# Weight sums of a Strassen-form MLP: one step per head behind a norm's power, in place of a fixed grid, and two sets moved from the recurrence to the first MLP

## The chip, the cores and the metric

The kernel runs on one core of a Trainium2 chip. The metric is the device time of one execution in microseconds (us), here the median of several runs. The names of the engines in profile rows: PE is TensorE (matmuls), PEld its weight loads, DVE is VectorE, ACT is ScalarE, POOL is GpSimd, SP is SyncE. DMAs are issued here by SP (queue q1 in the DMA view) and by POOL (queue q0); only POOL issues DMAs that add to what stands at their destination. A row like "L538" names line 538 of the kernel before; line 204 is a helper that issues every operation whose cost the kernel's planner counts, so L204 rows are told apart by their tiles.

## What is computed

One sequence of 1024 tokens, width 1024, runs through two layers: a gated linear recurrence with eight heads, an MLP of width 4096 with a squared ReLU, a causal convolution module, and a second such MLP, each followed by a layer norm of the weighted residual sum. All of it is float32.

```python
for i in range(DEPTH):                       # DEPTH = 2
    if i == 0: mix = hgrn2_mixer(x, ...)     # recurrence, 8 heads of 128
    else:      mix = conformer_conv_mixer(x, ...)
    x = layer_norm(ALPHA * x + mix, ...)
    ff = square(relu(x @ ffn_w1[i])) @ ffn_w2[i]
    x = layer_norm(ALPHA * x + ff, ...)
```

Within the recurrence each head's output is normed before it is gated: `o * rsqrt(mean(o*o) + RMS_EPS)`, per token and head.

## The kernel before

Matmuls are made of float32 operands cut into a high and a low part, three matmuls for each pair. The large products also use a Strassen form: a product of 2 x 2 blocks is made from seven products (`ORDER` lists them) of sums of blocks instead of eight. This takes sums of the weights' blocks. For the second matrix of each MLP (`ffn_w2`, cut into eight chunks per layer, each of four blocks of 128 x 1024) the sums are made in DRAM, by DMAs, long before the chunk is used. One **set** is the sums of one chunk, four tiles of 0.5 MB named sum_w. It takes two copies of 1 MB (`v[:, 0:2]` and `v[:, 2:4]`), one add of 1 MB onto the first two tiles, and two chained adds of 0.5 MB, each of which adds the tile before it to the next, so that each of the three adds can start only when an earlier DMA has landed. 4 MB are moved in a set. The list `to_sum` holds the sixteen sets, the eight of layer 0 first; layer 0's down product reads its sums from about 860 us on (dr<-sum_w), layer 1's at the end of the kernel.

The recurrence is written as one hand-made order for all engines. An outer loop goes over twelve pairs of projection blocks (`PAIRS`), seven products (`ORDER`) each, twelve matmuls a product; after each three matmuls `slot()` moves a counter of ticks on. Work is put off with `later(n, job)`: the job is recorded n ticks on, on whatever engines it uses. Between the products a generator per head, `recurrence(h)`, is stepped, so that a head's small matmuls stand between the large ones. Each head ends thus: `settle(0)` and `settle(1)`, one for each half of the tokens, take squares and their sums on ACT (L755), a scale and the power -1/2 on POOL (L756, then L538 in `power_m_half`), and, four ticks later, the scaling on ACT (L761), whose result PE transposes. Each engine works its instructions off in the order in which they are recorded. A DMA that POOL issues waits there until what it reads has landed, and all that is recorded behind it on POOL waits too.

In this kernel sets are given out by position: at every sixth product (`(7 * p + ORDER.index(i)) % 6 == 1`, L1042) while more than four sets are left, `block_sums` records the first copy, the second copy six ticks later, and the add and the two chained adds 12, 24 and 36 ticks later (`gap=12`). That gives twelve sets to the recurrence. Their lines are L419 and L420 (copies), L421 (add) and L423 (chained adds). Two more sets are made in the first MLP, after chunks 0 and 2, in seven pieces, one behind each form's product (`sum_pieces`): there the four tiles are copied one at a time by SP (L435), each behind a DMA of one element that holds it until the form is cut (L434), and the three adds are POOL's (L440). The last two are made in the second MLP (L413, L415).

The last head (7) has no tiles of its own for its values: it loads them into the halves of the finished tile F, named f, in the middle of its recurrence (`load_values(2 * h, F...)`, issued by SP at L652), while the earlier heads load theirs two heads ahead (tile v). The matmuls `ps<-f,kt` and `ps<-f,at` take f. Around this `seam()` loads the first matrix of the output projection (w_out, SP, L960, tile raw, cast at L952) and the stored heads (back<-zd, u<-od).

After the recurrence the order is no longer made by hand (`order.close()`): a scheduler that models the engines sets it. In the first MLP, `Forms.ahead(3)` keeps three cut forms of the weights (tile fw) ahead of PE; ACT casts the high part (L72), VectorE makes the low one. Beside this `spare` prepares later weights: POOL's one-element copies L1464 and L1472 gate the use of a tile that ACT casts (L1465, spare<-next), and SP stores the result (ready<-spare).

Of the kernel before, what the change touches and what calls it, by code (L numbers as in the profile page):

```python
# [8 lines left out]
F32 = mybir.dt.float32  # L9
# [3 lines left out]
ALU = mybir.AluOpType  # L13
PSUM = bass.MemoryType.PSUM

P = 128
# [3 lines left out]
H = 8  # L20
# [24 lines left out]
ORDER = (1, 2, 6, 5, 7, 3, 4)  # L45
# [223 lines left out]
def body(ctx, tc, d, out):  # L269
    nc = tc.nc  # L270
    cst = ctx.enter_context(tc.tile_pool(name="cst", bufs=1))
    stat = ctx.enter_context(tc.tile_pool(name="stat", bufs=4))
    dram = ctx.enter_context(tc.tile_pool(name="dram", bufs=1, space=bass.MemoryType.DRAM))
# [110 lines left out]
    def later(n, job):  # L384
        if n:
            waiting.append((ticks[0] + n, job))
        else:
            job()

    def tick(n=1):  # L390
        for _ in range(n):
            ticks[0] += 1
            for at, job in [w for w in waiting if w[0] <= ticks[0]]:
                waiting.remove((at, job))
                job()

    sums = {}

    def block_sums(name, layer, c, after=None, gap=0, adds=None):

        t = sums[name, layer, c] = dram.tile([4, P, 1024], F32, name=f"sum_{name}{layer}{c}")
        v, w = t.rearrange("a p n -> p a n"), d[name][layer, c].rearrange("a p n -> p a n")
        queue = nc.sync if after is not None else nc.gpsimd
        if adds is not None:

            def copies(rows, after):
                nc.sync.dma_start(out=t[0:4:2, rows.start, 0:1], in_=after)
                queue.dma_start(out=v[rows, 0:2], in_=w[rows, 0:4:2])
                queue.dma_start(out=v[rows, 2:4], in_=w[rows, 0:2])

            copies(slice(16, P), after)
            adds.append(lambda after: copies(slice(0, 16), after))
            adds.append(lambda after: nc.gpsimd.dma_start(out=v[:, 0:2], in_=w[:, 2:4], accum_op=ALU.add))  # L413
            for i in (2, 3):
                adds.append(lambda after, i=i: nc.gpsimd.dma_start(out=v[:, i], in_=v[:, i - 1], accum_op=ALU.add, max_dma_last_dim=4096))  # L415
            return
        if after is not None:
            nc.sync.dma_start(out=t[0:4:2, 0, 0:1], in_=after)
        queue.dma_start(out=v[:, 0:2], in_=w[:, 0:4:2])  # L419
        later(gap // 2, lambda: queue.dma_start(out=v[:, 2:4], in_=w[:, 0:2]))  # L420
        parts = [lambda: nc.gpsimd.dma_start(out=v[:, 0:2], in_=w[:, 2:4], accum_op=ALU.add)]  # L421
        for i in (2, 3):
            parts.append(lambda i=i: nc.gpsimd.dma_start(out=v[:, i], in_=v[:, i - 1], accum_op=ALU.add, max_dma_last_dim=4096))  # L423
        for i, part in enumerate(parts):
            later((i + 1) * gap, part)

    def sum_pieces(name, layer, c):

        t = sums[name, layer, c] = dram.tile([4, P, 1024], F32, name=f"sum_{name}{layer}{c}")
        v, w = t.rearrange("a p n -> p a n"), d[name][layer, c].rearrange("a p n -> p a n")  # L430

        def copy(i, q):
            def go(after):
                nc.sync.dma_start(out=t[i : i + 1, 0, 0:1], in_=after)  # L434
                nc.sync.dma_start(out=v[:, i], in_=w[:, q])  # L435

            return go

        def add(out, x, **kw):
            return lambda after: nc.gpsimd.dma_start(out=out, in_=x, accum_op=ALU.add, **kw)  # L440

        def chained(i):
            return add(v[:, i], v[:, i - 1], max_dma_last_dim=4096)

        return [copy(0, 0), copy(1, 2), add(v[:, 0:2], w[:, 2:4]), copy(2, 0), chained(2), copy(3, 1), chained(3)]

    to_sum = [(*of, c) for of in (("w2", 0), ("w2", 1)) for c in range(NFC)]
# [73 lines left out]
    for k in range(4):  # L521
        c = slice((k % 2) * HT, (k % 2 + 1) * HT)
# [14 lines left out]
    def power_m_half(dst, src, n):  # L537
        nc.gpsimd.tensor_tensor(out=dst, in0=src, in1=nhalf[:, :n], op=ALU.pow)  # L538
# [115 lines left out]
    def recurrence(h):  # L654
# [71 lines left out]
        for n in (32, 64):  # L726
            for s in range(0, n2, 2 * n):
                c, r = divmod(s, P)
# [22 lines left out]
        def settle(half):  # L751
            ss = stat.tile([P, 2, 4], F32, tag="ss", name="ss")
            cs = range(half * NTB, half * NTB + NTB)
            for c in cs:
                nc.scalar.activation(o[:, c], out_ps[:, c, :], AF.Square, scale=1.0 / QSCALE, accum_out=ss[:, 0, c % NTB : c % NTB + 1])  # L755
            nc.gpsimd.tensor_scalar(out=ss[:, 1], in0=ss[:, 0], scalar1=1.0 / P, scalar2=RMS_EPS, op0=ALU.mult, op1=ALU.add)  # L756
            power_m_half(ss[:, 0], ss[:, 1], 4)

            def rest():
                for c in cs:  # L760
                    nc.scalar.activation(o[:, c], out_ps[:, c, :], AF.Copy, scale=ss[:, 0, c % NTB : c % NTB + 1])  # L761
                later(1, lambda: ready.add(half))

            later(4, rest)
# [38 lines left out]
        def attend(cs):  # L803
            for c in cs:
                tensor.matmul(out_ps[:, c, :], A[:, c, :], values(c), start=True, stop=c == 0)
                if c:
                    tensor.matmul(out_ps[:, c, :], Q[:, c * P : (c + 1) * P], states[c], start=False, stop=True)
# [6 lines left out]
        later(1, lambda: (chain(range(NTB, nk)), settle(0)))  # L814
        yield
        attend(range(NTB, 2 * NTB))
        later(1, lambda: settle(1))
        if h < H - 2:
            for half in range(2):
                load_values(2 * h + 2 + half)  # L820
# [168 lines left out]
    def seam():  # L989
        plan = [  # L990
            (5, lambda: fetch(0, 0)), (15, lambda: split_w(0, 0, 136)), (17, lambda: split_w(0, 1, 144)), (19, lambda: split_w(0, 3, 120)),
            (21, lambda: split_w(0, 2, 152)), (13, lambda: heads_in(0, 0, 4, 32)), (19, lambda: heads_in(0, 4, 6, 32)),
            (24, lambda: split_heads(0, 0)), (26, lambda: split_heads(0, 2)), (29, lambda: split_heads(0, 4)),
            (16, lambda: bring(0)), (17, lambda: bring(1)), (27, lambda: last_in(H - 2, 0, sixth[0])), (36, lambda: last_in(H - 1, 0, lastly[0])),
            (21, lambda: heads_in(1, 0, 6, 64)), (38, lambda: split_heads(1, 0)), (41, lambda: split_heads(1, 2)), (44, lambda: split_heads(1, 4)),
            (25, lambda: fetch(1, 80)), (39, lambda: split_w(1, 0, 112)), (42, lambda: split_w(1, 1, 128)),
            (45, lambda: split_w(1, 2, 96)), (47, lambda: split_w(1, 3, 104)),
            (43, lambda: last_in(H - 2, 1, sixth[1])), (46, lambda: last_in(H - 1, 1, lastly[1])),
        ]
        for n, job in plan:  # L1000
            later(n, job)
# [25 lines left out]
    for p, (kind, j) in enumerate(PAIRS):  # L1027
        st = {"banks": dict(turn_of)}
        turn_of = {"z": turn_of["a"], "a": turn_of["b"], "b": turn_of["z"]}
        pace[1] = 0.0 if p == 0 else 0.6 if p < 3 else 0.5  # L1030
        if kind == "g" and p < len(PAIRS) - 1:
            to_load += [(2 * j, 0), (2 * j + 1, 1), (2 * j, 1), (2 * j + 1, 0)]
        if p == len(PAIRS) - 1:
            seam()
        for i in ORDER:
            if kind == "q" and i == 2:
                while any(a[0] <= j - 3 for a in active) or recs and recs[0] <= j - 3:
                    tick()
                    step()
            pair_product(p, i, made.pop(0), st)  # L1040
            later(2, make_form)
            if (7 * p + ORDER.index(i)) % 6 == 1 and len(to_sum) > 4:  # L1042
                block_sums(*to_sum.pop(0), gap=12)
        if kind == "q":
            later(4, lambda j=j: recs.append(j))
    early_out = ((0, 0), (1, 0), (2, 0))
# [9 lines left out]
    tick(100)  # L1056
    assert not waiting and not loaded and not to_load and not gates, (waiting, gates)
    order.close()
    oT = [o[0] for o in oT]


# [186 lines left out]
    class Up:  # L1248
# [14 lines left out]
        def settle(self, c):  # L1263

            for q in range(2):
                self.first(self.of[c], q)
# [224 lines left out]
    for c in range(NFC):  # L1491
        for i in ORDER[2 if c < 2 else 0 :]:
            (f,) = fw.take(1)
            fw.ahead(3)
            if (c, i) == (0, 7):
                bg.done()
            up.form(c, i, f)
            if summing:
                summing.pop(0)(f[:1, 1, :1].bitcast(F32))
        if c in (0, 2):  # L1500
            summing += sum_pieces(*to_sum.pop(0))
        if c == 0:
            up.settle(1)
            hold += [view(208, (2, 1024), F32, "spare"), view(216, (1024,), F32, "next")]
# [478 lines left out]
```

## Time and profile before

| what | value |
|---|---|
| time before, median of 3 runs | 2057.65 us (2055.35 to 2061.02) |
| the profiled execution's own time | 2057.38 us |
| its span, first to last instruction | 2055.6 us |
| granted clock of TensorE, mean | 0.998 |
| busy: POOL | 394.7 us, 405 instructions |
| DMA of SP's queue (q1) | 456.93 MB, 61.7% of 16 engines' span |
| DMA of POOL's queue (q0) | 58.72 MB, 12.3% |
| copies and adds of POOL from the weights, 1 MB each | 40, 10.8 us from issue to landing (median) |
| chained adds of POOL, 0.5 MB each | 32, 8.3 us |

How to read it: the profile is one execution, so sums are made against its own 2057.38 us, and the median of the runs is 0.27 us above that. PE's busy time is modelled, and a matmul's duration overlaps the next one's; idle time of PE is what an edit can gain. A row of waits tells which engine and tile waited for what: us in total, how often, the longest. A timeline row has start, duration, engine, line, operation, tiles, and in brackets the idle time before it with what ended it.

### The profile page before, as it was taken

What the parts mean: (1) busy time and instruction counts of PE and PEld (TensorE: products, weight loads), DVE (VectorE), ACT (ScalarE), POOL (GpSimd) and SP (SyncE); (2) the same over time, 40 slices, a digit from 0 to 9 for tenths busy, and PEclk for the clock granted to TensorE, in tenths of its full rate; (3) what the DMA queues carried; (4) which work ended last, traced back from release to release, by engine and by line L of the source; (5) the groups of instructions that cost most, each with busy time, mean ns of one, the idle gap of its engine ahead of it and who ended that gap; (6) DMA issues with size and microseconds to landing.
All of it is one profiled execution on the core that took longest, in us unless ns stands there. A gap on an engine that the chain in (4) does not pass through costs nothing. (4 is left out here: it accounts for less than half of the span.)

```text
span 2055.6 us, 29682 instructions
## 1 busy us (share of the span) xinstructions
PE 2024.2 (98%) x11144; PEld 1669.3 (81%) x11144; DVE 1488.7 (72%) x1978; ACT 1092.3 (53%) x1725; POOL 394.7 (19%) x405
## 2 busy tenths in 40 slices
PE   8999999999999999999999999999999999999998
PEld 7888887888788888888888888888888888888886
DVE  8698887877866665666557898889589666754456
ACT  5456565631654655444443776488615555443343
POOL 0112232111000000000001799079210000100002
PEclk9999999999999999999999999999999999999999
DMA  4788999942399786999998755487659778995542
GB/s 187 216 206 229 263 244 250 268 185 89 125 324 298 275 302 215 374 341 325 336 339 294 303 185 187 191 329 268 255 210 344 247 236 299 392 293 195 194 154 103
DMA packets 183120, 517.55 MB, mean 252 GB/s; under 512 B 17984, under 2 KB 49856, under 8 KB 181824
## 3 DMA queue, kind: packets, MB, share of 16 engines
q1 hardware_dynamic: 167488, 456.93, 61.7%
q0 software_dynamic: 15488, 58.72, 12.3%
q8 instruction: 87, 1.43, 0.3%
q14 instruction: 57, 0.47, 0.1%
HBM read 380.85 MB, written 201.85 MB: 283 GB/s over the span
## 5 line engine op out<-in xcount | busy, mean ns | idle before, releaser
L204 PE MATMUL ps<-dw,dh 128*128 128x512 f32 x2688 | 611.6, 389 | 0.9 <-ACT dh L72 0.7
L204 PEld LDWEIGHTS ps<-dw,dh 128*128 128x128 f32 x2688 | 504.1, 188 | 106.3 <-ACT dh L72 1.1
L204 PE MATMUL ps<-x1f,fw 128*128 128x512 f32 x1344 | 307.8, 390 | 4.3 <-ACT fw L72 2.9
L204 PEld LDWEIGHTS ps<-x1f,fw 128*128 128x128 f32 x1344 | 251.4, 188 | 59.2 <-issue 2.7
L204 PE MATMUL ps<-xf,fs 128*128 128x512 f32 x1008 | 250.0, 399 | 3.5 <-issue 1.9
L204 POOL TENSOR_TENSOR cb<-cb,prod 128x512 f32<-128x512 f32 x168 | 222.5, 1333 | 14.4 <-ACT prod L1614 4.1
L204 PEld LDWEIGHTS ps<-xf,fs 128*128 128x128 f32 x1008 | 184.8, 189 | 42.8 <-issue 2.1
L204 DVE TENSOR_TENSOR dh<-dh 128x1024 fp32r<-128x1024 f32 x112 | 136.3, 1222 | 109.6 <-ACT dh L72 106.5
L204 DVE SCALAR_TENSOR_TENSOR ps<-u,par,ps 128x512 f32<-128x512 f32 x296 | 205.9, 749 | 10.7 <-ACT ps L1626 9.3
L204 PE MATMUL ps<-xa,wa 128*128 128x512 f32 x864 | 203.6, 393 | 1.3 <-DVE xa L204 0.9
L72 ACT CAST dh<-dh 128x1024 fp32r<-128x1024 f32 x112 | 117.2, 1050 | 146.3 <-DMA dh<-hf 141.2
L204 DVE TENSOR_TENSOR dw<-dr,dw 128x1024 fp32r<-128x1024 f32 x112 | 136.2, 1222 | 76.2 <-ACT dw L72 75.5
L204 PEld LDWEIGHTS ps<-xa,wa 128*128 128x128 f32 x864 | 160.2, 188 | 35.1 <-DVE xa L204 1.3
L72 ACT CAST dw<-dr 128x1024 fp32r<-128x1024 f32 x112 | 117.1, 1052 | 134.7 <-PE ps L204 114.0
L1614 ACT ACTIVATE prod<-u,par 128x512 f32<-128x512 f32 x168 | 119.2, 725 | 35.4 <-POOL cb L204 34.8
L538 POOL TENSOR_TENSOR mv<-mv,nhalf 128x1 f32<-128x1 f32 x32 | 42.2, 1319 | 403.9 <-DVE mv L204 393.6
L204 PE MATMUL ps<-w,oT 128*128 128x512 f32 x384 | 89.9, 392 | 1.3 <-ACT oT L952 0.8
L204 PE MATMUL ps<-xb,wa 128*128 128x512 f32 x384 | 91.1, 393 | 0.0
L204 PE MATMUL ps<-vw,xf 128*128 128x512 f32 x336 | 79.4, 398 | 6.1 <-ACT vw L455 5.5
L204 PEld LDWEIGHTS ps<-w,oT 128*128 128x128 f32 x384 | 71.4, 188 | 16.6 <-ACT oT L952 1.2
L204 PEld LDWEIGHTS ps<-xb,wa 128*128 128x128 f32 x384 | 71.1, 188 | 14.4
L1465 ACT CAST spare<-next 128x1024 fp32r<-128x1024 f32 x38 | 39.9, 1051 | 78.0 <-DMA next<-in_wpw_dram 23.9
(252 smaller groups left out, 2915.3 us busy)
## 6 DMA issues: line engine op xcount, KB each, us to landing
wa<-ready SPq DMA_DIRECT2D x140, 512.0 KB, 4.4
dh<-hf SPq DMA_DIRECT2D x112, 512.0 KB, 4.7
sum_w<-in_w_dram POOLq DMA_DIRECT2D x40, 1024.0 KB, 10.8
ready<-spare SPq DMA_DIRECT2D x76, 512.0 KB, 5.0
raw<-in_w1q_dram SPq DMA_DIRECT2D x66, 512.0 KB, 4.6
dr<-sum_w SPq DMA_DIRECT2D x64, 512.0 KB, 7.4
hf<-ht SPq DMA_DIRECT2D x112, 256.0 KB, 6.1
dr<-in_w_dram SPq DMA_DIRECT2D x48, 512.0 KB, 6.9
```

The costliest lines, as they stand in the source:

```text
L72: self.nc.scalar.copy(out=slot[:, 0, c], in_=raw[:, c])
L204: return op(*args, **kw)
L538: nc.gpsimd.tensor_tensor(out=dst, in0=src, in1=nhalf[:, :n], op=ALU.pow)
L1465: nc.scalar.copy(out=slot[:, 0].bitcast(F32R), in_=raw)
L1614: nc.scalar.activation(tp, u[:, k : k + HT], AF.Copy, scale=tap(j, k))
```

## The change

The twelve sets that `block_sums` gave out by position become ten that `sum_step` gives out. Each call of `sum_step` first records the next add of every set under way (`running`), and then, with `new`, starts another: both copies at once, and its three adds put on the list for the next three calls. Four calls stand at the products 1, 3 and 5 of the first pair and the first of the second pair. From then on there is one call per head, recorded directly behind `settle(1)`, that is behind the power of the head's second norm; heads 0 to 5 start a set, heads 6 and 7 only go on with what is under way, and head 7 takes two steps. Of the six sets left, `sum_pieces` makes four in the first MLP, after chunks 0, 2, 3 and 4, instead of two. The last two are made as before. The sums themselves and all matmuls are the same, and PE's order is the same, instruction by instruction.

```diff
--- before.py
+++ after.py
@@ -423,6 +423,26 @@
             parts.append(lambda i=i: nc.gpsimd.dma_start(out=v[:, i], in_=v[:, i - 1], accum_op=ALU.add, max_dma_last_dim=4096))
         for i, part in enumerate(parts):
             later((i + 1) * gap, part)
+
+    running = []
+
+    def sum_step(new):
+        for parts in list(running):
+            parts.pop(0)()
+            if not parts:
+                running.remove(parts)
+        if not new:
+            return
+        name, layer, c = of = to_sum.pop(0)
+        t = sums[of] = dram.tile([4, P, 1024], F32, name=f"sum_{name}{layer}{c}")
+        v, w = t.rearrange("a p n -> p a n"), d[name][layer, c].rearrange("a p n -> p a n")
+        nc.gpsimd.dma_start(out=v[:, 0:2], in_=w[:, 0:4:2])
+        nc.gpsimd.dma_start(out=v[:, 2:4], in_=w[:, 0:2])
+
+        def chained(i):
+            return lambda: nc.gpsimd.dma_start(out=v[:, i], in_=v[:, i - 1], accum_op=ALU.add, max_dma_last_dim=4096)
+
+        running.append([lambda: nc.gpsimd.dma_start(out=v[:, 0:2], in_=w[:, 2:4], accum_op=ALU.add), chained(2), chained(3)])
     def sum_pieces(name, layer, c):
@@ -814,7 +834,7 @@
         later(1, lambda: (chain(range(NTB, nk)), settle(0)))
         yield
         attend(range(NTB, 2 * NTB))
-        later(1, lambda: settle(1))
+        later(1, lambda: (settle(1), sum_step(len(to_sum) > 6), h == H - 1 and sum_step(False)))
         if h < H - 2:
             for half in range(2):
                 load_values(2 * h + 2 + half)
@@ -1039,8 +1059,8 @@
                     step()
             pair_product(p, i, made.pop(0), st)
             later(2, make_form)
-            if (7 * p + ORDER.index(i)) % 6 == 1 and len(to_sum) > 4:
-                block_sums(*to_sum.pop(0), gap=12)
+            if p == 0 and ORDER.index(i) in (1, 3, 5) or (p, i) == (1, ORDER[0]):
+                sum_step(True)
         if kind == "q":
             later(4, lambda j=j: recs.append(j))
     early_out = ((0, 0), (1, 0), (2, 0))
@@ -1056,6 +1076,7 @@
     tick(100)
     assert not waiting and not loaded and not to_load and not gates, (waiting, gates)
     order.close()
+    assert not running and len(to_sum) == 6
     oT = [o[0] for o in oT]
@@ -1497,7 +1518,7 @@
             up.form(c, i, f)
             if summing:
                 summing.pop(0)(f[:1, 1, :1].bitcast(F32))
-        if c in (0, 2):
+        if c in (0, 2, 3, 4):
             summing += sum_pieces(*to_sum.pop(0))
         if c == 0:
             up.settle(1)
```

What this does to the order on POOL, at two places of the recurrence. First the stretch from head 5's norms to the first norm of head 6, before; an L756 with its L538 is a norm, in pairs for the two halves of a head, and the number in sum_w tells the sets apart:

```order
L421 DMA sum_w_3242<-in_w_dram 128x2x1024
L756 TENSOR_SCALAR ss<-ss 128x4
L538 TENSOR_TENSOR ss<-ss,nhalf 128x4
L756 TENSOR_SCALAR ss<-ss 128x4
L538 TENSOR_TENSOR ss<-ss,nhalf 128x4
L423 DMA sum_w_3242<-sum_w_3242 128x1024
L419 DMA sum_w_3502<-in_w_dram 128x2x1024
L420 DMA sum_w_3502<-in_w_dram 128x2x1024
L423 DMA sum_w_3242<-sum_w_3242 128x1024
L421 DMA sum_w_3502<-in_w_dram 128x2x1024
L423 DMA sum_w_3502<-sum_w_3502 128x1024
L756 TENSOR_SCALAR ss<-ss 128x4
```

The same engine after the change, from behind head 5's second power through both norms of head 6 (L776 is the old L756, L558 the old L538; L443 are chained adds, L445 the 1 MB add, L439 and L440 copies):

```order
L443 DMA sum_w_2241<-sum_w_2241 128x1024
L443 DMA sum_w_2565<-sum_w_2565 128x1024
L445 DMA sum_w_3066<-in_w_dram 128x2x1024
L439 DMA sum_w_3469<-in_w_dram 128x2x1024
L440 DMA sum_w_3469<-in_w_dram 128x2x1024
L776 TENSOR_SCALAR ss<-ss 128x4
L558 TENSOR_TENSOR ss<-ss,nhalf 128x4
L776 TENSOR_SCALAR ss<-ss 128x4
L558 TENSOR_TENSOR ss<-ss,nhalf 128x4
L443 DMA sum_w_2565<-sum_w_2565 128x1024
L443 DMA sum_w_3066<-sum_w_3066 128x1024
L445 DMA sum_w_3469<-in_w_dram 128x2x1024
```

Before, a set's adds follow each other on POOL within a stretch between two heads' norms, and one stands right ahead of a norm; after, no DMA stands between two norms of a head, no set appears twice behind the same norm, and behind head 6's second power stand two chained adds and a 1 MB add where one chained add stood. Behind head 7's second power, where nothing stood before, the end of the sums is now:

```order
L558 TENSOR_TENSOR ss<-ss,nhalf 128x4
L776 TENSOR_SCALAR ss<-ss 128x4
L558 TENSOR_TENSOR ss<-ss,nhalf 128x4
L443 DMA sum_w_3066<-sum_w_3066 128x1024
L443 DMA sum_w_3469<-sum_w_3469 128x1024 x2
```

The last of these three is the one DMA there that reads what the DMA just ahead of it writes. In the first MLP, POOL's order behind the two sets that were there before (L460 are the adds of the pieces, L1485 and L1493 the old gates L1464 and L1472):

```order
 L1485 COPY spare<-ss 128x1
 L1493 COPY next<-ss 128x1
+L460 DMA sum_w_6163<-in_w_dram 128x2x1024
 L1485 COPY spare<-ss 128x1
 L1493 COPY next<-ss 128x1
+L460 DMA sum_w_6163<-sum_w_6163 128x1024
 L1485 COPY spare<-ss 128x1
 L1493 COPY next<-ss 128x1
+L460 DMA sum_w_6163<-sum_w_6163 128x1024
 L1485 COPY spare<-ss 128x1
+L460 DMA sum_w_6437<-in_w_dram 128x2x1024
 L1493 COPY next<-ss 128x1
```

Six adds (the first four are seen here) now stand among these gates, and each waits on POOL for a landing with the next gate behind it.

## The prediction

> **What bounds the kernel now.** I read the page's busy table first, then TensorE's waits, then the stages that the change touches.
>
> ```profile
> span 2055.6 us, 29682 instructions
> PE 2024.2 (98%) x11144; PEld 1669.3 (81%) x11144; DVE 1488.7 (72%) x1978; ACT 1092.3 (53%) x1725; POOL 394.7 (19%) x405
> ```
>
> TensorE (PE) is busy for 2024.2 of 2055.6 us. The change adds and removes no matmul, so it can move the time only through the 31.4 us in which PE idles, or by adding to them. Two stretches are touched: the recurrence (100 to 450 us) and the first MLP (560 to 850 us). The table of windows (busy us by engine, then clock, DMA share, GB/s) gives for them:
>
> ```profile
> 100.00:450.00 350.00, 340.71 (x3603) 281.59 (x3602) 289.59 (x463) 209.18 (x485) 75.32 (x87) 1.00 0.86 242
> 560.00:850.00 290.00, 288.95 (x1273) 238.34 (x1272) 184.13 (x219) 161.39 (x233) 17.59 (x40) 1.00 0.85 288
> ```
>
> PE idles 9.3 us in the first and 1.1 us in the second. So a gain is bounded by 9.3 us, 0.45%, before any loss. Next, who causes these waits (us in total, times, longest):
>
> ```profile
> PE ps L204 <- ACT vw L455: 5.5, 1, 5.5
> PE ps L204 <- ACT o L761: 2.4, 3, 1.1
> PE ps L204 <- issue: 1.9, 1, 1.9
> PE ps L204 <- DVE state L204: 1.4, 2, 0.9
> ACT o L761 <- POOL ss L538: 11.5, 8, 3.2
> POOL sum_w L423 <- DMA sum_w<-in_w_dram: 106.0, 12, 13.0
> ```
>
> The first four are PE's (the 5.5 us fall into the start), the fifth ScalarE's (ACT), the last GpSimd's (POOL), both between 75 and 425 us. POOL stands 106 us behind adds that have not landed; in three cases of the sixteen a norm's power (L538) queued behind them, ACT's scaling (L761) came late and PE waited, 2.4 us in all. Head 6 shows one such case, in the timeline:
>
> ```profile
> 380.62 0.86 POOL L423 DMA_DIRECT2D sum_w<-sum_w  x1 [10.90 <-DMA sum_w<-in_w_dram]
> 381.55 0.74 POOL L756 TENSOR_SCALAR ss<-ss 128x4 f32<-128x4 f32 x1
> 386.43 1.01 POOL L538 TENSOR_TENSOR ss<-ss,nhalf 128x4 f32<-128x4 f32 x1
> 387.39 0.88 POOL L423 DMA_DIRECT2D sum_w<-sum_w  x1
> ```
>
> **The change part by part.**
>
> *The norms are freed.* After the change a head's DMAs stand behind its second power, and each add's source was issued a head earlier (some 35 us), so POOL waits for no landing between two norms. The 2.4 us go: **-2.4**. It can be nothing less; at most the waits on state (1.4) and on a late ACT copy go as well, some -5.
>
> *PE's stop at 345 us.* The wait "issue" is a stop in which no semaphore is shown, and the clock drops behind it:
>
> ```profile
> 344.00:347.80 3.80, 1.91 (x10) 1.42 (x9) 0.62 (x2) 2.34 (x13) 1.43 (x3) 0.99 1.05 222
> 347.80:351.20 3.40, 3.40 (x12) 2.71 (x11) 1.71 (x4) 2.99 (x9) 1.12 (x2) 0.50 1.06 231
> ```
>
> It costs 1.9 us and half of 3.4 us, 3.6 in all. It falls into a stretch with DMA share 1.05; after the change POOL's DMA queue should be empty there, as the next part shows. Whether that cures it the trace can't say, so I take half: **-1.8**, ends 0 and -3.6.
>
> *The bursts.* Per head five DMAs of 4 MB in all are now issued in a row, some 1 us each. By the prices found below they are two adds of 0.5 MB (6.3 us of the engines), one of 1 MB (5.5) and 2 MB of copies (5.2): 17 us, and 29 us at the 56 parts in 95 that POOL's queue gets beside SP's. The heads are further apart, and other loads had to wait before too:
>
> ```profile
> L538 POOL TENSOR_TENSOR ss<-ss,nhalf x16: 1006/1027/1481, 153.1 to 413.7; 128x4 f32<-128x4 f32 x16
> v<-vd SPq DMA_DIRECT2D x14, 256.0 KB, 9.9
> ```
>
> (413.7 - 153.1) / 7 = 37 us a head. For heads 0 to 5 I cost the bursts at nothing: what they delay are loads of blocks and values that already took 9.9 us beside POOL's queue, and the lists of VectorE's and ACT's waits between 75 and 425 us hold no DMA. If that cover is gone, VectorE stops in order, and PE loses what exceeds the four forms in store, a few us.
>
> *Head 6's burst meets head 7's values.* This is the largest term. Behind head 6's second power stood one add of 0.5 MB (387.39 above); now stand two of 0.5 MB and one of 1 MB. Just then SyncE (SP) asks for what PE needs next:
>
> ```profile
> 391.24 2.25 SPq L960 DMA_DIRECT2D raw<-in_wout_dram  x4
> 394.02 0.57 SPq L652 DMA_DIRECT2D f<-vd  x1
> 403.94 1.16 PE L204 MATMUL ps<-f,kt 128*128 128x128 f32 x8
> 408.04 0.79 PE L204 MATMUL ps<-f,kt 128*128 128x128 f32 x5
> DMA to landing us min/median/max: 3.0/9.9/11.3
> ```
>
> The last row is that of the line that issues f<-vd (L652), for the v loads among it, whose landing the trace tells. 394.02 + 9.9 = 403.9 is exactly when PE takes f, without a wait: there is no reserve to be counted on. What the added DMAs cost the engines comes from the DMA view of four windows (queue: packets, MB, share of 16 engines): 380.6 to 386, a 0.5 MB add alone; 312.9 to 326, a 1 MB add with loads beside it (two rows); 395 to 404, loads alone.
>
> ```profile
> q0 software_dynamic: 144, 0.52, 58.3%
> q0 software_dynamic: 381, 1.43, 56.2%
> q1 hardware_dynamic: 1258, 1.76, 38.6%
> q1 hardware_dynamic: 1591, 3.58, 103.4%
> ```
>
> The 0.5 MB add takes 0.583 x 5.4 = 3.15 us of all 16 engines. In the second window q0 takes 0.562 x 13.1 = 7.4 us for 1.43 MB, 5.2 us a MB, so a 1 MB add (1.05 of these MB) takes 5.5. Added work: 3.15 + 5.5 = 8.65 us, in front of 395 to 404 us, where SP's queue alone fills the engines. Nothing hides it but the holes between 388 and 395 us, about half a us, and a burst that starts some 1 us earlier because the first norm isn't late any more. In the mixed window q0 got 56 parts to 39, so the adds are done long before f. PE then stops about 8.65 - 1.5, **+7.0**; ends 0 (f had more reserve than its median says) and +8.7. The second half of f shifts by as much and costs little more; ACT and VectorE stop with PE.
>
> [...]
>
> *The clock behind that stop.* After 1.9 us of idling came 3.4 us at half clock (above), after the longest wait of the run, the 5.5 us on ACT vw, none:
>
> ```profile
> 0.00:50.00 50.00, 44.48 (x184) 35.86 (x185) 41.60 (x56) 28.15 (x41) 0.79 (x8) 1.00 0.51 192
> ```
>
> I take half of 1.7: **+0.9**, ends 0 and 1.7. [...]
>
> *Head 7.* Two more adds of 0.5 MB, then a third, start behind its second power near 414 us, 3 x 3.15 = 9.5 us of work beside the second half of w_out, which ACT casts here:
>
> ```profile
> 413.54 1.90 SPq L960 DMA_DIRECT2D raw<-in_wout_dram  x4
> 425.43 1.04 ACT L952 CAST w<-raw 128x1024 fp32r<-128x1024 f32 x1
> 429.74 2.00 ACT L952 CAST w<-raw 128x1024 fp32r<-128x1024 f32 x2
> raw<-in_wout_dram SPq DMA_DIRECT2D x8, 512.0 KB, 7.0
> ```
>
> Issued from 413.5 us on, at 7.0 to landing and 1.3 us more for each that queues (0.52 MB at 3.58 MB in 9 us), they land from 420.5 to 424.4, some 5 us ahead of their casts; the first two adds (6.3 us) overrun that a little. **+0.5**, ends 0 and +4.
>
> *Two more sets in the first MLP.* Each is 2 MB of copies on SP's queue (at the 3.58 MB in 9 us above, 5.2 us) and 2 MB of adds (at 5.5 us a MB, 11 us), 33 us for both. In their stretch stand
>
> ```profile
> 660.00:780.00 120.00, 119.15 (x524) 98.01 (x524) 84.35 (x100) 69.65 (x103) 7.05 (x16) 1.00 0.79 272
> ACT spare L1465 <- POOL spare L1464: 17.7, 5, 8.9
> PE ps L204 <- DVE c L204: 0.9, 1, 0.9
> ```
>
> 0.21 x 120 = 25 us are free, so the engines fill up till about 790 us. POOL now waits for landings ahead of more of its gates L1464, ACT's spare cast behind them holds ACT up (17.7 us between 640 and 770, 8.9 at once), and yet PE lost 0.9 us to VectorE and none to that from 560 to 850. The code keeps three forms cut ahead of PE, 72 matmuls or 16 us (120 / 524 us each). I take **+0.5**, ends 0 and +6 (an ACT stop of 15 us where 8.9 cost nothing).
>
> **The sum.** The profiled execution took 2057.38 us, its span and 1.8 around it; that is 0.3 below the median of 2057.65. 2057.4 - 2.4 - 1.8 + 7.0 + 0.9 + 0.5 + 0.5 = **2062.1, so 2062 us**, 0.2% above the median.
>
> **Rivals.** *f arrives in time (0.27).* For it: its 14 sisters landed in as little as 3.0 us, and no row shows this very landing. Against it: they met a less full queue than 103.4%. Then the gains stand alone: 2057.4 - 2.4 - 1.8 + 1.0 = 2054, and 2051.4 when the stop at 345 us goes wholly.
>
> *The seam is bound by DMA (slower, 0.17).* Head 6's adds are wholly ahead of f (+8.7), the clock drops (+1.7), and head 7's adds hold back w_out (+4), while the stop at 345 us stays: 2057.4 - 2.4 + 8.7 + 1.7 + 4 = 2069. It decides from f landing later than 411 us; for it speaks that the queue of SP is full from 395 to 430 us, against it that SP's own issues move back with PE and so find it emptier.
>
> *ACT behind POOL in the first MLP (0.05).* If POOL's waits add up to more than PE's banks cover, +6 with a mild seam: 2064.
>
> *The change doesn't do what it says (0.03):* five DMAs in a row fill POOL's queue, POOL stands in an issue until the next head's norm, and the L761 waits remain, 2062 to 2065.
>
> **How the numbers follow.** The forecast, a stop of 4 to 8 us, has 0.48 and its own range is 2058 to 2066. 0.3% is about what a measurement of this kernel can tell from no change; on the median it is 6.2 us, 2051.5 to 2063.8. Faster by more than that needs f in time and most of the 9.3 us: 0.06, out of the first rival. Slower: the second rival whole (0.17), a third of the forecast (0.15) and 0.03 of the rest: 0.35. Within: 0.59. The range takes in the first rival and most of the second: 2052 to 2068.
>
> **What would show it.** Right: L423's follower behind L538 in every head, ACT's wait for POOL ss near 0, no PE wait on ACT o L761; PE idle 5 to 8 us ahead of the first matmul on f,kt, released by DMA f<-vd; a slice at half clock near 410 us or none; PE idle from 560 to 850 us under 2 us. Wrong: no wait on f<-vd, or a wait on raw<-in_wout larger than it, or PE waits on ACT c in the first MLP.

## The result, and the profile after

| | us, median | lowest to highest |
|---|---|---|
| before (6 runs beside it) | 2057.06 | 2055.35 to 2061.02 |
| after (6 runs) | 2068.39 | 2064.67 to 2069.06 |

The measured ratio is 1.0048 (95% interval 1.0036 to 1.0060); that of the two medians alone is 1.0055. By the medians the change makes the kernel 11.3 us slower, 6.4 us more than the forecast of 2062.0 and 0.4 us above the top of its range. The profiled execution of after took 2069.06 us. Its page begins:

```profile
span 2067.3 us, 29719 instructions
PE 2026.8 (98%) x11144; PEld 1671.8 (81%) x11144; DVE 1488.5 (72%) x1978; ACT 1092.0 (53%) x1725; POOL 386.5 (19%) x401
```

TensorE does the same 11144 matmuls and idles 40.5 us of the span where it was 31.4. Its list of waits, after (us in total, times, longest):

```profile
PE ps L204 <- DMA f<-vd: 5.4, 1, 5.4
PE ps L204 <- ACT vw L475: 5.1, 1, 5.1
PE ps L204 <- ACT c L1307: 3.8, 2, 2.7
PE ps L204 <- ACT fw L72: 2.9, 2, 1.5
PE ps L204 <- DVE t L204: 2.6, 3, 1.7
PE ps L204 <- ACT t L877: 1.4, 2, 0.9
...
PE ps L204 <- ACT o L781: 0.4, 1, 0.4
```

Against before, the wait on o is down from 2.4 to 0.4, as forecast, and "issue", whose end was given half a chance, is gone; f<-vd heads the list. But ACT c is there, which the prediction named as a sign of being wrong: from 560 to 850 us TensorE idles 3.8 us, where less than 2 was expected. DVE t with ACT t (first products) was not expected at all. ScalarE's and GpSimd's waits between 75 and 440 and between 75 and 430 us say why:

```profile
ACT fs L654 <- DMA pr<-in_wp_dram: 5.9, 1, 5.9
ACT o L781 <- POOL ss L558: 3.5, 5, 1.0
```

```profile
POOL ss L776 <- ACT o L775: 141.7, 16, 24.7
POOL sum_w L440 <- issue: 55.5, 8, 7.9
POOL sum_w L445 <- issue: 47.7, 9, 7.9
POOL sum_w L439 <- issue: 22.5, 9, 3.3
```

All 16 norms (L776) wait for ScalarE's squares alone, never for a landing. ScalarE waits 3.5 us for POOL's powers where it was 11.5, but 5.9 us for one load of a block. POOL's three "issue" rows come to 126 us: the DMAs of a head don't go out in a row. The sign of it stood in the trace of before, between 75 and 425 us, and the prediction passed over it:

```profile
POOL sum_w L421 <- issue: 38.7, 7, 6.2
```

Where the 11.7 us between the two profiled spans arise is read by the start of the same matmul (the n-th of its group) in both traces: its lag in the other kernel, at nine places and at the end. The table gives the growth of that lag from place to place; the experiments below are in it too, each by one profiled execution, with the median of its runs less that of before beside it.

| us, against before | to 98 | 98-125 | 125-335 | 335-355 | 355-392 | seam, 392-425 | 425-520 | 520-860 | 860-1450 | 1450-end | median |
|---|---|---|---|---|---|---|---|---|---|---|---|
| after | -0.4 | +3.2 | -1.3 | -3.7 | -1.1 | +8.8 | 0 | +3.1 | -0.5 | +3.6 | +11.3 |
| seam_drop | -0.4 | +3.1 | -1.2 | -3.6 | -1.1 | 0 | 0 | +3.8 | -1.7 | +0.1 | -0.6 |
| no_1mb | +0.1 | +2.6 | -1.5 | -3.6 | -1.2 | +2.4 | 0 | +1.1 | -1.5 | +1.7 | +3.3 |
| f_early | +0.3 | +2.9 | -1.4 | -3.6 | -1.0 | +5.9 | 0 | +2.4 | -0.7 | +1.4 | +5.7 |
| spread4 | -0.2 | +2.2 | -1.3 | -3.6 | -1.1 | +9.0 | 0 | +0.6 | -0.1 | -0.2 | +7.1 |
| start_gated | +0.3 | 0 | -1.2 | -3.7 | -1.1 | +8.6 | 0 | +6.3 | +0.6 | +1.0 | +5.6 |
| mlp_two | -0.3 | +2.4 | -1.4 | -3.6 | -1.1 | +9.5 | 0 | -2.8 | -0.5 | +1.6 | +4.5 |
| before_mlp4 | +0.4 | 0 | +3.9 | -3.6 | -1.1 | -0.1 | 0 | +0.7 | -0.6 | +0.8 | -0.2 |
| late_adds | +0.6 | +4.4 | -1.3 | -3.6 | +15.3 | -0.2 | 0 | +1.9 | -0.1 | +0.3 | +17.8 |
| all_moved | +21.2 | 0 | -1.2 | -3.6 | +16.4 | -0.2 | 0 | -2.0 | +0.3 | +0.2 | +32.4 |
| tail_adds | -0.9 | 0 | -1.3 | -3.6 | -1.1 | +0.2 | +2.7 | -0.6 | +0.8 | +1.9 | -2.2 |
| two_behind_norms | -0.1 | 0 | -1.2 | -3.7 | -1.1 | 0 | +11.1 | -2.2 | -1.4 | +0.1 | +5.9 |
| three_plus_three | +1.1 | 0 | -1.2 | -3.6 | -1.1 | 0 | 0 | +1.4 | -0.7 | -0.2 | -2.4 |

From 98 to 520 us most columns repeat within 1 us wherever two kernels share the code. Two don't: late_adds has 4.4 at 98 to 125 us, with a stretch of half clock at 126 us that the others lack, and before_mlp4 has 3.9 at 125 to 335 us, where POOL's order is still that of before. Behind 520 us the columns scatter by some us, as the runs do, whose times spread over 4 to 11 us in most kernels. A profiled execution can also lie off its median: that of start_gated took 2068.05 us (median 2062.46), that of two_behind_norms 2058.86 us (2062.39). So the early columns can carry a verdict by a single trace where the difference is well over 1 us, and the late ones only by several kernels together.

### The profile page after: what moved, and what is told of

It reads as the page before. It is cut to its first block, busy times and chain, and to the rows that moved or that the text cites. A ratio compares the mean times of both kernels' runs of the same rounds, so it can differ in the third digit from the quotient of the medians.

```text
span 2067.3 us, 29719 instructions
## 1 busy us (share of the span) xinstructions
PE 2026.8 (98%) x11144; PEld 1671.8 (81%) x11144; DVE 1488.5 (72%) x1978; ACT 1092.0 (53%) x1725; POOL 386.5 (19%) x401
## 4 chain that ended last, share of the span: by engine, by line
PE 70%; DMA 11%; DVE 10%; issue 4%; ACT 3%; POOL 2%; SPq 1%; DVEq 0%; POOLq 0%; ACTq 0%
PE ps L204 70%; DMA hf<-ht 3%; DMA raw<-in_w1q_dram 2%; POOL cb L204 1%; DVE fw L204 1%; DMA next<-in_wpw_dram 1%; DMA dh<-hf 1%; DVE t L204 1%; DVE qk L204 1%; DMA vr<-in_wv_dram 1%; DMA f<-vd 1%; DVE ht L204 1%; DMA hf<-hr 1%; DMA pr<-in_wp_dram 1%; DVE c L204 1%
## 5 line engine op out<-in xcount | busy, mean ns | idle before, releaser
L72 ACT CAST dh<-dh 128x1024 fp32r<-128x1024 f32 x112 | 117.3, 1050 | 147.1 <-DMA dh<-hf 141.8
L72 ACT CAST dw<-dr 128x1024 fp32r<-128x1024 f32 x112 | 117.1, 1052 | 139.7 <-PE ps L204 121.9
L558 POOL TENSOR_TENSOR mv<-mv,nhalf 128x1 f32<-128x1 f32 x32 | 42.2, 1320 | 390.8 <-DVE mv L204 380.4
L204 PEld LDWEIGHTS ps<-vw,xf 128*128 128x128 f32 x336 | 64.3, 192 | 20.4 <-ACT vw L475 5.1
## 6 DMA issues: line engine op xcount, KB each, us to landing
sum_w<-in_w_dram POOLq DMA_DIRECT2D x36, 1024.0 KB, 10.3
```

The source lines that it names most:

```text
L72: self.nc.scalar.copy(out=slot[:, 0, c], in_=raw[:, c])
L204: return op(*args, **kw)
```

## The experiments

**The seam.** In after, POOL's timeline and then SP's show, from head 6's second power on (start, us, what; in brackets the idle time ahead):

```profile
381.99 1.01 POOL L558 TENSOR_TENSOR ss<-ss,nhalf 128x4 f32<-128x4 f32 x1
382.95 1.83 POOL L443 DMA_DIRECT2D sum_w<-sum_w  x2
389.20 1.17 POOL L445 DMA_DIRECT2D sum_w<-in_w_dram  x1 [4.42 <-issue]
```

```profile
388.48 2.33 SPq L980 DMA_DIRECT2D raw<-in_wout_dram  x4
...
393.41 0.53 SPq L672 DMA_DIRECT2D f<-vd  x1
```

The trace has the landing of these: the 1 MB add at 403.4, 14.2 us after its issue, f at 406.8, and TensorE starts on f at 406.97 behind 5.4 us of idling. At the end of that stop the clock falls; the windows of after:

```profile
400.00:405.60 5.60, 1.58 (x8) 0.99 (x6) 2.35 (x2) 1.63 (x2) 0.00 (x0) 1.00 1.04 351
405.60:409.00 3.40, 2.03 (x9) 2.06 (x10) 0.00 (x0) 1.91 (x3) 0.00 (x0) 0.56 1.04 417
409.00:412.40 3.40, 3.40 (x12) 2.82 (x11) 2.47 (x5) 0.79 (x1) 0.00 (x0) 0.50 0.96 324
```

Two stretches of 3.41 us at half speed, where one was priced at half a chance. Three kernels take this apart. The first leaves head 6's three adds out:

```diff
-            parts.pop(0)()
+            part = parts.pop(0)
+            if not leave_out:        # True for head H - 2
+                part()
```

> Head 6's three adds (0.5, 0.5 and 1 MB) are left out, so three of the weight sums are wrong. Theory (the added adds take the DMA engines just ahead of f<-vd): TensorE's wait of 5.4 us on f<-vd falls under 1 us and the 3.4 us that the half clock cost behind it go too: 8.8 us off, about 2059.6 us. Rival (f<-vd is late because four loads of w_out stand ahead of it on SyncE's queue, and it never had a reserve): the wait stays above 3 us and the time above 2064.

Measured: 2056.47 us, ratio to before 0.9993 (0.9979 to 1.0006). The seam costs 0.0 and TensorE has no wait on f<-vd; its 8.8 us are the adds'. The rival falls. That the median came down by 11.9 and not by 8.8 lies in the last columns, as far as single traces show it. The second leaves out the 1 MB add alone (`len(parts) == 2` in that branch):

> Of head 6's three adds only the one of 1 MB is left out (issued at 389.20 and landed at 403.40 us before), so one weight sum is wrong. Theory (what f<-vd loses is the engine time of the bytes still under way behind 393 us, 5.5 us for this add): the wait of 5.4 us falls under 1 us, no half clock follows, the seam (392 to 425 us) gives back 8.8 us: 2056.5 to 2059.6 us. Rival (the two adds of 0.5 MB, 6.3 us of engine time, do half of it by pushing the loads of heads and w_out back): 2 to 3 us of the wait stay, with 1.7 us of half clock, 2062 to 2064.

Measured: 2059.80 us, 1.0018 (1.0008 to 1.0028). Its waits on f are down to

```profile
PE ps L204 <- DMA f<-vd: 0.9, 1, 0.9
```

with no half clock, and the seam costs 2.4 in place of 8.8. So leaving out this one add, which in after goes out behind the two small ones, takes away 4.5 of the 5.4 us and all of the half clock; 0.9 us stay with the two small adds alone, less than the rival's 2 to 3. The 1 MB add without the small ones wasn't tried. The third keeps all adds and issues f sooner:

```diff
         total(4)
         total(8)
+        if h == H - 1:
+            load_values(2 * h, F[:, :HT]...)
+            load_values(2 * h + 1, F[:, HT:]...)
```

(and the two loads at their old places go)

> Nothing left out; the two loads of head 7's values are issued as soon as the buffer f is free, ahead of w_out's four loads. Theory (f is late in the queue): the wait on f<-vd goes, 5.4 + 3.4 = 8.8 us off, about 2059.6 us. Rival (the engines are full, so that what f gains the loads of w_out and of the heads lose): a wait on ACT w or DVE oT of 3 us or more takes its place, and the time stays above 2064.

Measured: 2062.79 us, 1.0027 (1.0015 to 1.0039). The wait on f is gone, and between 390 and 425 us these two stand in its place, with a stretch of half clock behind the first (396.5 to 399.9 us):

```profile
PE ps L204 <- DVE blocks L204: 2.8, 1, 2.8
PE ps L204 <- ACT kt L765: 1.8, 1, 1.8
```

The seam costs 5.9 in place of 8.8: the DMA engines are full (share 0.99 to 1.08 from 392 to 403 us), and what f gains, others partly lose. This is nearer to the rival in kind, though neither wait is the one it named and the time is 1.2 us below its bound.

**The first calls.** In after, the block loads that SP issued from 88.7 to 92.7 us landed from 103.0 to 105.2 us (96.4 to 97.7 before) and were wanted at 97; that is ScalarE's 5.9 us on pr above. First the calls were set further apart, with `if 7 * p + ORDER.index(i) in (1, 7, 13, 19):`.

> Nothing left out; the first four calls stand after the products 1, 7, 13 and 19 in place of 1, 3, 5 and 7. Theory (three sets at once in 100 to 130 us delay the loads of blocks, so that PE waits for VectorE's t): the 3.2 us lost between 100 and 125 us go, about 2065.2 us. Rival (the same bytes then meet the heads, which lose as much): the 3.2 us turn up between 150 and 300 us and the time stays within 1 us of the changed kernel's 2068.4.

Measured: 2064.17 us, 1.0032 (1.0019 to 1.0045). The median is near the forecast, yet not for its reason: 2.2 of the 3.2 us stay (the kernels that leave the first calls alone have 2.4 to 4.4), and the gain is in the late columns. POOL's timelines, of before and of after, explain it:

```profile
80.01 1.22 POOL L421 DMA_DIRECT2D sum_w<-in_w_dram  x1 [4.78 <-DMA sum_w<-in_w_dram]
94.18 0.86 POOL L423 DMA_DIRECT2D sum_w<-sum_w  x1 [12.96 <-DMA sum_w<-in_w_dram]
```

```profile
79.89 1.22 POOL L445 DMA_DIRECT2D sum_w<-in_w_dram  x1 [5.05 <-DMA sum_w<-in_w_dram]
84.46 0.71 POOL L439 DMA_DIRECT2D sum_w<-in_w_dram  x1 [3.35 <-issue]
```

Before, the wait for the set's own landing held POOL from 81 to 94 us. After, the next set's copies stand between an add and its successor, and nothing on POOL waits for TensorE there, so the "product" behind which a call stands sets the order on POOL and no time. The second trial ties them:

```diff
+            if at in (1, 7, 11, 15):          # at = 7 * p + ORDER.index(i)
+                if at > 1:
+                    nc.gpsimd.tensor_copy(out=now, in_=f[:, 1, :1].bitcast(F32))
+                sum_step(True)
```

> Nothing left out; the first four calls stand at the products 1, 7, 11 and 15, and ahead of the last three POOL copies one column of the form that this product uses, so that it can't run ahead of TensorE by more than the forms in store. Theory (POOL's DMAs were tied to nothing there: it issued from 73 us on as fast as its queue took them, L439 at 84.46 us where it stood until 94.18 us before the change, and so the block loads used at 97 us landed at 105 us): the block loads issued from 88 to 93 us land by 99 us, the 3.2 us lost between 98 and 125 us fall to 1 us or less, about 2065.5 us. Rival (the load there is the same whenever it is issued, as in the run with the calls at 1, 7, 13 and 19): 2 us or more stay lost there.

Measured: 2062.46 us, 1.0028 (1.0018 to 1.0038). POOL now stands 23 us (releaser: the form's cut), the block loads land by 95.2 us, and the column from 98 to 125 us is 0. Of the 5.9 us between the medians of after and of this kernel, these 3.2 are placed and the rest is not:

```profile
98.64 0.18 POOL L1067 COPY ss<-fs 128x1 f32<-128x1 f32 x1 [23.13 <-DVE fs L204]
98.95 1.21 POOL L445 DMA_DIRECT2D sum_w<-in_w_dram  x1
```

**The first MLP.** VectorE's waits between 690 and 745 us, before and then after:

```profile
DVE ht L204 <- DMA hf<-ht: 4.2, 3, 3.0
```

```profile
DVE ht L204 <- DMA hf<-ht: 17.6, 4, 7.5
```

VectorE stands in order behind its own stores, adds c late, ScalarE waits for c, TensorE for ScalarE. This chain is read from the waits. In the next kernel the two extra sets are left out (they read another set's sums).

> The two extra sets of the first MLP are left out (their places read another set's sums, which makes the result wrong). Theory (their 8 MB of DMA delay VectorE's stores hf<-ht, VectorE then adds c late): the 4.6 us that TensorE lost between 690 and 745 us, with the half clock behind them, go: about 2063.8 us, and VectorE's waits for hf<-ht between 690 and 745 us fall from 17.6 us to the 4.3 us or so seen before the change. Rival (the loss there comes from the later start of the stage, which moved the work of the queues against each other): the loss stays, 2067 or more.

Measured: 2061.55 us, 1.0016 (1.0006 to 1.0027); VectorE's wait there is

```profile
DVE ht L204 <- DMA hf<-ht: 4.6, 3, 3.3
```

and 520 to 860 us gives -2.8 in place of +3.1. The opposite trial puts two more sets there in the kernel before: `c in (0, 2, 3, 4)`, `len(to_sum) > 6`.

> The kernel before with the last two sets of the recurrence moved into the first MLP (four sets in pieces there), nothing else of the change. Theory (two more sets cost 5 to 6 us there, whatever the recurrence does): 5 us more between 640 and 860 us, less about 1 us of a late norm of head 6: about 2061 us. Rival (the loss in the first MLP is only of the changed kernel's shifted stages): within 1.5 us of the kernel before, 2057.1.

Measured: 2056.64 us, 0.9998 (0.9988 to 1.0009): this theory fails. The stage costs 0.7, though VectorE waits 8.9 us for hf<-ht. So the price isn't fixed. The ten traces with four sets there give -0.6 to +6.3 in this column, mean 2.1; the four with two sets (before is 0 by definition) -2.8 to 0, mean -1.8. About 4 us in the mean, and a spread as large. Part of the spread is the clock: six of the fourteen traces have a stretch of half clock in it, 3.4 us long and so worth up to 1.7 us (after and start_gated at 741 us, four others between 533 and 553 us). What else decides wasn't found.

This kernel shows two more things, in the early columns. At 268 us POOL stands longer in the issue of an add than in before's trace (there 4.3 us), with a norm behind it:

```profile
267.83 1.22 POOL L421 DMA_DIRECT2D sum_w<-in_w_dram  x1 [6.50 <-issue]
269.12 0.19 POOL L756 TENSOR_SCALAR ss<-ss 128x4 f32<-128x4 f32 x1
```

TensorE waits 3.7 us for ACT o L761, where before's trace has 1.1, a stretch of half clock follows, and the column has 3.9. So what the change cures is real, but at this place, in the same order, it cost 1.1 us in one execution and more than three times that in another. And the stop at 345 us is absent here too.

**Moving what collides.** Two kernels set head 6's and 7's six adds, and in the second two whole sets, behind the norms of the output projection: `after_norm()` issued them in x1_block, the second also with the gated start and `c in (0, 2)`. (The 21 MB of the second's text are a slip: six adds are 3.5 MB, two sets 8 MB more.)

> Nothing left out; the six adds of heads 6 and 7 are issued behind the norms 4 to 6 of the output projection, from 478 us on, where the DMA engines were busy for 0.22 of the time. Theory: TensorE's wait on f<-vd goes under 1 us and no half clock follows, as in the run without head 6's adds; 8.8 us less at the seam, and no new wait between 445 and 560 us: 2059.6 us or, with what the shifted stages gave there as well, 2056.5. Rival (the adds slow the loads of forms between 500 and 560 us, or POOL's norms behind them): 3 us or more are lost between 480 and 560 us, 2062 or above.

> Nothing left out; the gated start, heads 6 and 7 without adds, their six adds and two whole sets behind the eight norms of the output projection (453 to 519 us), two sets in the first MLP as before the change. Theory, from the stages of the runs so far: 0 to 1 us lost at the start, 6 us won by the norms and the stop at 345 us, nothing lost at the seam, nothing in the first MLP: about 2051 to 2052 us, faster than both. Rival (the 21 MB that now pass the DMA engines from 453 to 530 us hold the loads of forms ahead of the first MLP): the 6 us are lost again between 500 and 580 us, 2057 or more.

Measured: 2074.62 us, 1.0081 (1.0068 to 1.0094), and 2089.24 us, 1.0153 (1.0140 to 1.0166). Neither did what its edit meant. Behind the recurrence, whose order is written out by hand, the scheduler places instructions, and these DMAs from one part of DRAM to another depend on no engine's work: it moved the adds up to 368 us, ahead of head 6's norms, and the two sets to 1.3 us. As POOL's timeline of late_adds shows, the norm then stands behind landings, and TensorE waits 14.6 us for ACT o:

```profile
381.64 0.86 POOL L443 DMA_DIRECT2D sum_w<-sum_w  x1 [3.15 <-DMA sum_w<-sum_w]
388.41 0.81 POOL L443 DMA_DIRECT2D sum_w<-sum_w  x1 [5.91 <-DMA sum_w<-in_w_dram]
389.30 0.19 POOL L776 TENSOR_SCALAR ss<-ss 128x4 f32<-128x4 f32 x1
395.67 0.82 POOL L443 DMA_DIRECT2D sum_w<-sum_w  x1 [6.18 <-DMA sum_w<-sum_w]
396.24 1.33 POOL L558 TENSOR_TENSOR ss<-ss,nhalf 128x4 f32<-128x4 f32 x1
```

That is what the change removes, at its dearest. The next three keep the order by hand: gated start, no adds behind heads 6 and 7, and at the recurrence's end a POOL copy of w_out's last cast piece with the adds behind it.

```diff
+    nc.gpsimd.tensor_copy(out=now, in_=ws[1][3][:, 1, :1].bitcast(F32))
+    for _ in range(3):
+        sum_step(False)
     order.close()
```

> Nothing left out; the gated start, no adds behind heads 6 and 7, and the six adds that are left in program order at the end of the recurrence, behind a copy by POOL of the last cast piece of w_out (some 436 us). Theory: nothing lost at the start and at the seam, 6 us won before it as in the earlier runs, no wait between 445 and 560 us though POOL's first norm there comes up to 12 us late; the four sets in the first MLP cost 1 to 7 us, as in the runs so far: 2052 to 2058 us. Rival (the late norms hold up the projection): 3 us or more lost between 445 and 580 us, 2059 or above.

Measured: 2054.29 us, 0.9994 (0.9981 to 1.0007). Start and seam cost 0 and 0.2; POOL's first norm of the projection comes at 448 us behind the adds, and one wait of TensorE follows:

```profile
PE ps L204 <- DVE y L204: 2.5, 1, 2.5
```

The same with the two extra sets as `sum_pieces(...)` tied to the norms' results, and `c in (0, 2)`:

> Nothing left out; as the run with the six adds at the end of the recurrence, and the two extra sets go in pieces behind the norms of the output projection, tied to these norms' results, so that the first MLP has two sets as before the change. Theory: 0 at the start, 6 us won before the seam, 0 at the seam, nothing lost in the first MLP: about 2051 us, faster than both. Rival (pieces on POOL stand ahead of its norms and the projection's chain waits, or the loads of forms at 500 to 560 us come late): 3 us or more lost between 445 and 580 us, 2054 or above.

Measured: 2062.39 us, 1.0024 (1.0014 to 1.0035): the rival. POOL's norms stand behind pieces that wait (10.3 us at 473 us), and TensorE waits between 445 and 520 us for

```profile
PE ps L204 <- DVE x1f L204: 7.0, 2, 5.3
```

with two stretches of half clock, 11.1 us in all; the first MLP's 2.2 us don't pay for it. Last, the six adds split: three behind head 7's second power, three behind the copy (`h != H - 2 and sum_step(h < H - 2)`, `range(2)`).

> Nothing left out; as the run with the six adds at the end of the recurrence (2054.3 us), but the first three of them go out behind head 7's second power (some 407 us), where three adds stood in the changed kernel without a loss behind 425 us, and three behind the copy (some 429 us). Theory (the 2.7 us that TensorE lost there between 445 and 520 us came from POOL's first norm standing behind landings until 448 us): that norm comes by 443 us, the 2.7 us go, about 2051.6 us, and the kernel is faster than the one before by 0.2%. Rival (the three adds at 407 us hold back the second half of w_out, or head 7's values): 2 us or more lost between 405 and 450 us, 2054 or above.

Measured: 2053.05 us against 2055.45, 0.9984 (0.9969 to 0.9999). The 2.7 us are gone, nothing is lost at 405 to 450 us, and this is the one kernel whose interval lies below 1: its median is 2.4 us below that of before beside it, where the changed kernel's was 11.3 us above. The interval just tells that from no change, and one such among thirteen kernels may be chance.

## Why the prediction was right, and where not

- **The norms, -2.4**: -1.3 and -1.1 at 125-335 and 355-392 us, -2.4. Right in size. The three waits behind it were not of one kind, though: 0.9 us at 385 us stood behind a landing (the late power there is the one at 382.38 us, which the prediction's lines leave out; 386.43 is the other half's), 1.1 us at 268 us stood behind the issue of an add, at which POOL stood for 4.3 us, and 0.4 us at 159 us behind neither. This last one is still there in after.
- **PE's stop at 345 us, -1.8**: -3.7, in every kernel run. The windows of after at that place have no slice at half clock and half the DMA share of before's 1.05:

```profile
344.00:348.00 4.00, 4.00 (x114) 3.41 (x105) 2.15 (x5) 3.17 (x14) 1.63 (x3) 1.00 0.52 145
348.00:352.00 4.00, 4.00 (x83) 3.26 (x81) 3.04 (x7) 3.60 (x9) 2.07 (x3) 1.00 0.76 143
```

  Half a chance was too little. The lower share fits the prediction's reason, but no kernel varies it alone, and the trace doesn't tell what TensorE stood for. That the stop is in every run of before rests on its one trace.
- **f<-vd, +7.0, and the clock, +0.9**: the lag grows by 8.8 where these and head 7's 0.5 make 8.4. The mechanism is shown by seam_drop. Within it the wait was smaller (5.4) and the clock dearer: with 0.9 us on DVE blocks ahead of the stop, some 2.5 us are left for it. That there was no reserve is right: in before f landed at 403.2 us and TensorE took it at 403.9. But of the 5.4 us only some 3.6 are f's later landing (406.8 us); some 2.4 are TensorE's own earlier arrival (401.6 us), which the gains ahead of the seam had brought and which the sum left out, less 0.7 of reserve. Counted in packets, SP's queue passed far more than POOL's: from 390.4 to 403.4 us, while the 1 MB add was under way, 917 of SP's beside 337 of POOL's, and 1258 beside 381 in the prediction's mixed window. "Five DMAs in a row" is wrong too: the third add went out 6.3 us behind the first, when the first had landed (5.9 us after its issue). Whether f would have been spared by an add issued at 385 us wasn't tried.
- **Half a chance for the clock**: it was taken because no fall was seen behind the 5.5 us wait at the start of before. That is a misreading. The first record of the clock in that trace is at 9.8 us, and a view shows time without a record as full clock; behind that wait the matmuls ps<-vw,xf follow each other every 427 ns up to 9.8 us and every 227 ns soon after, 9 in the first stretch below against 21 in the second, so they ran at about half speed:

```profile
5.40:9.70 4.30, 4.23 (x9) 3.13 (x10) 2.19 (x4) 1.96 (x5) 0.00 (x0) 1.00 0.98 327
9.90:14.20 4.30, 4.30 (x21) 3.53 (x20) 3.71 (x7) 3.39 (x7) 0.00 (x0) 1.00 1.03 420
```

- **Head 7, +0.5**: nothing is lost behind the seam up to 520 us.
- **The bursts, at nothing: this step failed.** For the heads it holds (nothing lost from 125 to 392 us, no wait on blocks or values). The first four calls it passed over: their bursts got no price of their own, and they cost 3.2 us. The cover that the step named, loads that land late anyway, ends at 97 us, where blocks are wanted that land at 105; and what it put down for a cover gone, "a few us", was due. start_gated shows it.
- **Two more sets in the first MLP, +0.5**: +3.1, inside the ends 0 and 6, about 4 in the mean of kernels. Its chain (POOL's gates, then ACT's spare) was the wrong one: between 640 and 770 us ACT's wait for these gates fell from 17.7 to 9.5 us. The wait that stands there is VectorE's, for its own stores, and up to 1.7 us more went to a stretch of half clock at 741 us, for which the sum had no term. The rival that priced this stage at +6 had 0.05.
- **Behind 1450 us, no term**: +3.6 in after, mostly in five waits on VectorE of 0.4 to 1.1 us, against three of 0.2 to 0.7 in before; -0.2 to +1.9 in all other kernels. No experiment puts it down to a part of the change; it stays open.

Of the rivals, f in time falls with the wait of 5.4 us (its lower time is 2052.4 by its own terms, not 2051.4). The seam bound by DMA gives 2069 and so nearly the measured time, but not by its parts: f landed at 406.8 and not behind 411 us, w_out held nothing up, and the stop at 345 us went. POOL did stand in issues, 126 us at L440, L445 and L439 together, and yet no norm came late for it; that its queue was full there was not shown.

So the forecast of a slower kernel, by a stop at the seam, was right, and its sum too small. Between the profiled spans it lacks 7.0 us (11.7 against 4.7): 3.2 at the start, 2.6 in the first MLP, 3.6 behind 1450 us, less 1.9 at 345 us, and the rest in tenths.

## What to carry to other kernels

Here POOL's DMAs, tied to nothing, were paced by its own waits alone: with the wait for a landing gone they ran ahead to where nobody placed them (the next set's copy went out at 84.46 us in after, where POOL had stood until 94.18 us before). So an edit that moves an issue "behind" a piece of work has to give it a data dependency on that work, or a hand-written order on an engine that waits for it. Before paying bytes into a stretch, look for the loads that have no reserve there (here f and the blocks wanted at 97 us) and keep the stretch just ahead of them free. A delay cost more than itself where the clock fell behind it: in before 3.4 us at half clock behind a stop of 1.9 us, in after 6.8 us at half clock behind 5.4 us. And read the "issue" rows of the engine that issues: in the kernel before they showed POOL standing at L421 for 38.7 us, where the trace shows no semaphore that it waited for.

## What the runs showed of the hardware that was not expected

- POOL didn't issue its DMAs without a stop. In after, with two adds of 0.5 MB under way, it stood 4.42 us in the issue of a 1 MB add, till one of the two had landed (two from 382.95 us, the first landed 5.9 us later, the third at 389.20, above), while in before a 0.5 MB add and two 1 MB copies went out in a row, from 353.38 to 354.71 us, as its timeline shows:

```profile
353.38 0.94 POOL L423 DMA_DIRECT2D sum_w<-sum_w  x1 [4.38 <-DMA sum_w<-in_w_dram]
353.99 1.07 POOL L419 DMA_DIRECT2D sum_w<-in_w_dram  x1
354.71 1.06 POOL L420 DMA_DIRECT2D sum_w<-in_w_dram  x1
```

  So a count of DMAs alone doesn't explain it; what does was not measured. Before had such stops too, the 38.7 us at L421 above.
- The clock fell for one stretch of 3.41 us behind stops of 1.9 us (before, 345 us) and 2.7 us (after, 740 us), for two behind 5.4 us (after, 406 us), and not at all behind 2.5 us (tail_adds). Length alone didn't decide: one wait of 1.5 us for ACT fw L72, between 531 and 571 us, is in all fourteen traces, and four of them have a fall behind it. In three_plus_three the wait ends at 532.7 us and there follows

```profile
533.40:536.80 3.40, 3.40 (x10) 2.63 (x9) 3.40 (x4) 0.90 (x2) 2.24 (x1) 0.50 0.43 159
```

  In after the two falls begin 334.5 us apart, 98 times 3.413 (the clock records of the two traces give a fall 3.413 us in before, and 6.827 and 3.413 us in after), and in late_adds two are 262.8 us apart, 77 times. The stretch at full clock ahead of the first fall, 337.92 us in before and 395.95 us in after, is 99 and 116 times that. So in these three traces the stretches lie on a grid; what sets it, and how long a stop must be ahead of a fall, was not measured.
